# A hybrid MLA/NSA decoder in two layers: a third tile for the split weights, last down slabs in other buffers, and an earlier start of the gates

## The chip, the cores and the metric

The kernel runs on one core of a Trainium2 chip, as one program of 12504 matmuls. The metric is the device time of one execution in microseconds. The engines are named as in the profile: PE is TensorE, DVE is VectorE, ACT is ScalarE, POOL is GpSimd and SP issues transfers.

## The reference

The input is 512 tokens of width 1024. Each of two layers adds half a SwiGLU network, a token mixer, and half a second SwiGLU network; layer 0 mixes by multi-head latent attention (MLA), layer 1 by native sparse attention (NSA). One norm stands at the end.

```python
def rmsnorm(x, g):
    y = x * lax.rsqrt(jnp.mean(x * x, axis=-1, keepdims=True) + RMS_EPS)
    return y * g

def swiglu(x, w_gate, w_up, w_down):          # 1024 -> 2816 -> 1024
    return (jax.nn.silu(x @ w_gate) * (x @ w_up)) @ w_down

h = x
for i in range(2):
    h = h + 0.5 * swiglu(rmsnorm(h, ffn_norm_a[i]), ...)
    m = rmsnorm(h, mix_norm[i])
    h = h + (mla_mixer(m, ...) if i == 0 else nsa_mixer(m, ...))
    h = h + 0.5 * swiglu(rmsnorm(h, ffn_norm_b[i]), ...)
return rmsnorm(h, final_norm)
```

MLA projects to a latent of 384 for queries and 256 for keys and values, norms both, expands them to 16 heads of 64 + 32 (rotary) and applies a causal softmax. NSA has 16 heads in four groups and adds three gated branches: attention over compressed blocks of 32 tokens (an MLP over each block), over selected blocks, and over a causal window of 512 with a relative bias.

## The kernel before

**Precision and splits.** Every product is computed in fp32r (a reduced form of fp32 for PE) on values split in a high and a low part: ACT writes the high part (a copy into fp32r), DVE or POOL writes the low part (the value less the high part), and three matmuls make one product: high by high, high by low, low by high. So every weight slab that comes from memory goes through one ACT and one DVE or POOL instruction before PE may use it. `split` (L165 on) does that for activations, `wslab` (L131 on) for weights: SP loads the slab into a raw buffer `wr` (two of them), L144 writes the high part, L146 (DVE) or L150 (POOL) the low one. Both parts lie in one tile `w` from `wtiles`; there are two such tiles, by a counter, so slab number k can be written only when the matmuls that read slab k-2 are done. While `lo_pool` is set, in the two attention stages, the low parts of weights are POOL's, in pieces of up to 512 columns.

**The FFNs.** There are four, by stage a0 (5.7 to about 335 us in the trace before), b0 (546 to 895), a1 (898 to 1225) and b1 (1543 to 1860); `idx` 0 to 3 is their number. `ffn` runs over 22 blocks of 128 hidden units. The first three are "plain": 48 matmuls of 128x256 for the gate (`pg`, L365 to L367) and 48 for the up projection (`pu`). The other 19 form sums of weights and of activations (`combine`, `wsums`, `product`) and need seven products where eight stand in the plain form; the sums are DVE's work, and their tiles are `fr` (raw), `fh` and `fl` (high and low), three of each. The down projection runs in units of three blocks between those (`unit`, tiles `wdr`, `wd`), and what is left of it, the last four blocks, comes at the end of the stage, one slab of 128x512 for each of eight chunks of the residual `h`. Those eight slabs go through `wslab`, so through `wr` and `w`. In the last FFN another function, `last`, does that end.

**The norm at the start of an FFN.** The products are made of the unnormed `h`, and the norm's factor comes in afterwards. After the first plain block, `norm_col` sums squares on PE into `pc`, then a chain of twelve small DVE instructions on 128x4 (L260 to L272, the name `small`) computes the reciprocal root; `norm_bcast` (L291) spreads it over the partitions by PE into `pb`, ACT copies it to `row`, and `gate` and `act` multiply with it. All engines work in order, so PE waits at `pb` if the chain on DVE is not done.

**The attention stages.** In MLA (335 to 546 us) `query` multiplies a projection by a table into `tq` and splits it (L172) into tiles `four` and `q`; scores `s` follow, then a softmax whose last scaling is POOL's (L772), transposes `pt` and the product with the values. The output of a head pair is split into `oh` and `ol`, the low part by POOL. In NSA (1230 to 1540 us) POOL scales `p` (L1091) and the compressed branch's `e` (L1053), copies the compressed values into `vcm` (L1013), splits `ohl`, and splits the weights (L150). So POOL's queue is one list in which weight splits stand between pieces of softmax. `pp` are projections on PE, `pv` values, `ptc` the transposes of `e`.

**What sets the order.** The program is written through a tile framework. A scheduler in it puts the instructions of each engine in order by priorities and by when buffers come free. `issue_after` and `high_priority` change that. So a change of a buffer count moves instructions on every engine.

```python
t = self.first or self.wp.tile([P, 2048 + 3 * PAD], F32R, tag=f"w{self.nw % 2}", name="w")   # L128
raw = self.wp.tile([P, 1024], F32, tag="wr", bufs=2, name="wr")                              # in wslab
```

Of the kernel before, what the change touches and what calls it, by code (L numbers as in the profile page):

```python
# [11 lines left out]
F32 = mybir.dt.float32  # L12
F32R = mybir.dt.float32r
I32 = mybir.dt.int32
AF = mybir.ActivationFunctionType
# [3 lines left out]
P = 128  # L19
S = 512  # L20
D = 1024
KC = D // P
FF = 2816
NF = FF // P
EPS = 1e-6
NEG = -1e30
H = 16
# [21 lines left out]
KP = KC // 2  # L49
PLAIN = 3  # L50
PAD = 16
TILES = 24
XC = P + 2
NG = 3
# [4 lines left out]
def f32v(ap):  # L59
    return ap.bitcast(F32)  # L60


class Kern:
# [13 lines left out]
    def setup(self):  # L77
# [4 lines left out]
        self.nw, self.odd, self.nq = 0, 0, 0  # L82
        self.first = self.wp.tile([P, 2048 + 3 * PAD], F32R, tag="w0", name="w")
        small = self.wp.tile([P, 80], F32, name="small")
# [40 lines left out]

    def wtiles(self, kind="x"):

        t = self.first or self.wp.tile([P, 2048 + 3 * PAD], F32R, tag=f"w{self.nw % 2}", name="w")  # L128
        self.nw, self.first = self.nw + 1, None
        o, d = {"x": (0, 0), "act": (3 * PAD, 0), "half": (PAD, 2 * PAD)}[kind]  # L130
        return t[:, o : o + 1024], t[:, o + d + 1024 : o + d + 2048]  # L131
# [139 lines left out]
            nc.vector.tensor_tensor(t, t, y, op=ALU.mult)  # L271
            nc.vector.scalar_tensor_tensor(y, t, 1.5, y, op0=ALU.add, op1=ALU.mult)  # L272

    def norm_col(self, n, s2, pool=False):

        nc = self.nc
        pc = self.bank("o", "pc")
        for i in range(4):
            nc.tensor.matmul(pc[:, i : i + 1], s2[:, i * P : (i + 1) * P], f32v(self.ones)[:, 0:1], start=True, stop=True)
        return self.rsqrt_col(pc[:, 0:4], n, pool)  # L280

    def rsqrt_col(self, s, n, pool=False):
        v, t, col = self.vtc[:, 0:4], self.vtc[:, 4:8], self.vtc[:, 8:12]
# [85 lines left out]
    def ffn(self, idx, gain_next, ap, tp):  # L369
        nc, a = self.nc, self.a  # L370
        self.scr, self.fp = (tp, "sq", 1), tp
        ah, al, ht, row = {}, {}, [], None
        tg, tu, units = {}, {}, []

        def gate(f, g):

            t = tg[f] = tp.tile([P, S], F32, tag="tg", bufs=2, name="tg")
            nc.vector.tensor_tensor(t, g, row, op=ALU.mult)
            nc.scalar.activation(t, t, AF.Silu, scale=-1.0)
            nc.vector.tensor_tensor(t, t, row, op=ALU.mult)  # L380
# [4 lines left out]
        def act(f):  # L385
            t = tu[f]
            if f < PLAIN:
                t = tu_tile()
                nc.vector.scalar_tensor_tensor(t, tu[f], -1.0, tg[f], op0=ALU.mult, op1=ALU.mult)
            else:  # L390
                nc.vector.tensor_tensor(t, t, tg[f], op=ALU.mult)
            ah[f] = ap.tile([P, S], F32R, tag="act", bufs=4 * NG, name="ah")
            al[f] = ap.tile([P, S], F32R, tag="act", bufs=4 * NG, name="al")
            self.split(t, ah[f], al[f])

        def down(p, w, b0, b1):
            for k in range(b0, b1):
                last = self.mm3(p, w[0][:, k - b0], w[1][:, k - b0], ah[k], al[k], k == b0, k == b1 - 1)
            return last
# [27 lines left out]
                tokens(t)  # L427


        gates = [self.bank("T", "pg") for _ in range(PLAIN)]  # L430
        for f, g in enumerate(gates):
            u = tu[f] = self.bank(("mm", "S")[f % 2], "pu")
            self.plain(idx, f, 0, g)
            if f == 1 and idx == 0:

                squares(0)
                tokens(3)
                squares(1)
            if f == 2:
                pb = self.norm_bcast(col)  # L440
                row = tp.tile([P, S], F32, tag="row", bufs=1, name="row")
                nc.scalar.activation(row, pb, AF.Copy)
                for e in range(2):
                    gate(e, gates[e])
                    act(e)
            self.plain(idx, f, 1, u)
            if f == 0 and idx:
                for c in self.late:
                    self.sumsq(self.h[c])
                col = self.norm_col(D, self.s2)  # L450
            elif f == 1 and idx == 0:
                squares(2)
                squares(3)
                col = self.rsqrt_col(sums, D)
            elif f == 2:
                gate(f, g)
                act(f)
            for p in (((0,), (1,), (2, 3)) if idx else ((0, 1), (2,), (3,)))[f]:
                self.combine(p)
        t = self.tiny  # L460
# [3 lines left out]
        tail = PLAIN + (NF - 2 - PLAIN) // NG * NG  # L464
        for f in range(PLAIN, NF):
# [3 lines left out]
            n = -(-len(units) // left)  # L469
            left -= 1  # L470
            todo, units = units[:n], units[n:]
            w = self.wsums(idx, f)
            x, q, g = self.bank("S", "px")[:, :HS], self.bank("mm", "pq")[:, :HS], self.bank("T", "pg")
            uq = tp.tile([P, S], F32, tag="uq", bufs=1, name="uq")
            t = tu[f] = tu_tile()
# [18 lines left out]
        if gain_next == "fin":  # L494

            hs, out = [self.parts(self.four(F32)) for _ in range(4)], []
            for t in range(4):
                for b in range(2):
                    p = self.mm_bank("ph")
# [5 lines left out]
        self.norm_begin(gain_next)  # L505
        for c in self.order:
            p = self.mm_bank("pd")
            down(p, self.wslab(a["w_down"][idx, c, :, tail * P :], (NF - tail, P), "act"), tail, NF)
            add(c, p)
            self.norm_chunk(c)  # L510

# [130 lines left out]
    def mla(self, gain_next):  # L642
        nc, tc, a = self.nc, self.tc, self.a
        with ExitStack() as cx:
            mp = cx.enter_context(tc.tile_pool(name="mla", bufs=1, reuse_waits="tile"))
            tp = cx.enter_context(tc.tile_pool(name="mlat", bufs=2, reuse_waits="tile"))
# [12 lines left out]
            pb = self.norm_bcast(self.norm_col(D, self.s2))  # L659
            row = tp.tile([P, S], F32, tag="row", bufs=1, name="row")  # L660
# [35 lines left out]
            for k in range(2):  # L696
                nc.vector.tensor_tensor(ckv[k], ckv[k], rkv, op=ALU.mult)
                hi, lo = ckvp[2 * k : 2 * k + 2]
# [4 lines left out]
            p = self.proj(a["mla_w_in"][5], P, xh, xl, "pr")  # L703
# [47 lines left out]
            def query(h, w=None):  # L751
                p = self.proj(None, P, cqh, cql, "pq", w or query_slab(h))
                t = tp.tile([P, S], F32, tag="tq", bufs=2, name="tq")
                nc.vector.tensor_tensor(t, p, cst, op=ALU.mult)
                qh, ql = self.qtile(), self.qtile()
                self.split(t, qh, ql, pool=True)
                return qh, ql

            qs, oh, ol, o32 = {}, [], [], [None]
# [15 lines left out]
            def end(h):  # L775
                o = self.bank("o", "o")
                self.pv(o, pth[h % 2], ptl[h % 2], lambda j: vt[j][h // 4][:, h % 4, :], True, True)
                if h % 2 == 0:
                    o32[0] = tp.tile([P, S], F32, tag="o32", bufs=2, name="o32")
                self.o_out(o, o32[0], h % 2, tp)  # L780
                if h % 2 == 1:
                    hi = tp.tile([P, S], F32R, tag="o", bufs=12, name="oh")
                    lo = tp.tile([P, S], F32R, tag="o", bufs=12, name="ol")
                    self.split(o32[0], hi, lo, pool=True)
                    oh.append(hi)
                    ol.append(lo)

                if h == 0:
                    vals(1)
                if h % 2 == 1 and h + 3 < H:  # L790
                    keys((h + 3) // 2)
                if h >= 8 and h % 2 == 0:
                    self.w_o(a["mla_w_o"][0], oh[:4], ol[:4], [h // 2 - 4], False)

            w = self.wslab(a["mla_w_k"][0:2].rearrange("a p c -> p a c"), (2, 2, P))
# [538 lines left out]
```

## Time and profile before

| | |
|---|---|
| median of 3 runs | 1894.92 us (1894.47 to 1899.17) |
| the profiled execution, its own time | 1895.84 us |
| its span, first to last instruction | 1894.1 us |
| mean granted clock of PE | 0.998 |
| PE busy | 1865.5 us, 98% |
| DVE busy | 1527.9 us, 81% |
| ACT busy | 1088.9 us, 57% |
| POOL busy | 244.7 us, 13% |
| read from memory | 178.96 MB, 96 GB/s over the span |
| transfers | two hardware queues (72800 and 2944 packets); no software queue in the list |

The span is what the trace covers; the time of the execution is 1.74 us longer. A row of the trace names its line of code, engine, operation and tiles, and in brackets how long the engine was idle before it and what ended that. DVE's low parts (L146, L172) and POOL's (L150, L172) are the same operation on two engines.

### The profile page before, as it was taken

Reading aid. Unit: us, or ns where it says so; the run is one execution under the profiler, and the core shown is the slowest. Engines: PE = TensorE matmul, PEld = TensorE weight load, DVE = VectorE, ACT = ScalarE, POOL = GpSimd, SP = SyncE. Lnnn points to the kernel's source line nnn. Section 1 sums busy time; section 2 is a strip of 40 time slices with the busy share of each in tenths; the row PEclk is TensorE's granted clock in tenths of the full one; section 3 lists DMA queues with packets and bytes.
Section 4 is the critical chain, followed back from the end, with each engine's and each line's share of the span. In section 5 each row is a group of like instructions: output and inputs, shape, how many; then the busy total and the mean of one; then the engine's idle time right before and its main releaser. Section 6 shows DMA issues by size and latency. Waiting matters only on the chain.

```text
span 1894.1 us, 32916 instructions
## 1 busy us (share of the span) xinstructions
PE 1865.5 (98%) x12504; PEld 1695.8 (90%) x12504; DVE 1527.9 (81%) x2913; ACT 1088.9 (57%) x2024; POOL 244.7 (13%) x334
## 2 busy tenths in 40 slices
PE   8999999999999999999999999999989999999998
PEld 8999999878889999998999999888778889999997
DVE  8988886677778888886898878666978988888885
ACT  8555554478765555554654555436867865555553
POOL 0000000047710000000000000015656600000000
PEclk9999999999999999999999999999999999999999
DMA  6433331311132333322333332143121133333321
GB/s 237 131 101 100 102 100 41 112 53 46 60 132 90 124 101 101 102 79 86 130 124 108 105 105 75 55 141 102 51 71 64 43 115 111 111 107 104 104 77 67
DMA packets 75902, 183.26 MB, mean 97 GB/s; under 512 B 9040, under 2 KB 37072, under 8 KB 75744
## 3 DMA queue, kind: packets, MB, share of 16 engines
q1 hardware_dynamic: 72800, 176.39, 29.4%
q10 hardware_dynamic: 2944, 4.77, 0.7%
q8 instruction: 98, 1.61, 0.4%
q14 instruction: 60, 0.49, 0.1%
HBM read 178.96 MB, written 2.16 MB: 96 GB/s over the span
## 4 chain that ended last, share of the span: by engine, by line
PE 86%; DVE 6%; ACT 4%; POOL 2%; issue 1%; DMA 0%; POOLq 0%; SPq 0%; DVEq 0%; ACTq 0%
PE pd L164 8%; PE pd L165 8%; PE pd L163 8%; PE px L353 5%; PE px L354 5%; PE px L355 5%; PE pg L353 4%; PE pg L354 4%; PE pg L355 4%; PE pq L354 3%; PE pq L353 3%; PE pq L355 3%; PE o L1139 1%; PE po L164 1%; PE po L165 1%; PE po L163 1%
## 5 line engine op out<-in xcount | busy, mean ns | idle before, releaser
L164 PE MATMUL pd<-al,wd 128*128 128x512 f32 x576 | 225.3, 391 | 0.0
L163 PE MATMUL pd<-ah,wd 128*128 128x512 f32 x576 | 224.9, 390 | 0.0
L165 PE MATMUL pd<-ah,wd 128*128 128x512 f32 x576 | 224.6, 390 | 0.0
L172 DVE TENSOR_TENSOR w<-wr,w 128x1024 fp32r<-128x1024 f32 x72 | 88.2, 1224 | 123.9 <-ACT w L171 123.9
L353 PE MATMUL px<-four,wh 128*128 128x256 f32 x608 | 168.8, 278 | 0.6 <-ACT pg L478 0.6
L355 PE MATMUL px<-four,wl 128*128 128x256 f32 x608 | 168.0, 276 | 0.0
L354 PE MATMUL px<-four,wh 128*128 128x256 f32 x608 | 167.9, 276 | 0.0
L353 PE MATMUL pq<-four,wh 128*128 128x256 f32 x608 | 167.8, 276 | 0.0
L354 PE MATMUL pq<-four,wh 128*128 128x256 f32 x608 | 167.8, 276 | 0.0
L355 PE MATMUL pq<-four,wl 128*128 128x256 f32 x608 | 167.8, 276 | 0.0
L144 ACT ACTIVATE w<-wr 128x1024 fp32r<-128x1024 f32 (+5 forms) x120 | 100.7, 845 | 113.7 <-issue 25.7
L171 ACT ACTIVATE wd<-wdr 128x384 fp32r<-128x384 f32 x192 | 99.3, 519 | 98.5 <-ACT wd L171 59.1
L402 DVE SCALAR_TENSOR_TENSOR h<-pd,h 128x512 f32<-128x512 f32 x216 | 147.9, 685 | 6.9 <-PE pd L165 6.8
L165 PEld LDWEIGHTS pd<-ah,wd 128*128 128x128 f32 x576 | 108.2, 188 | 22.8
L163 PEld LDWEIGHTS pd<-ah,wd 128*128 128x128 f32 x576 | 108.1, 188 | 20.5
L164 PEld LDWEIGHTS pd<-al,wd 128*128 128x128 f32 x576 | 108.1, 188 | 19.7
L172 DVE TENSOR_TENSOR wd<-wdr,wd 128x384 fp32r<-128x384 f32 x192 | 106.1, 555 | 16.3 <-ACT wd L171 15.6
L146 DVE TENSOR_TENSOR w<-wr,w 128x1024 fp32r<-128x1024 f32 (+4 forms) x81 | 80.7, 998 | 45.1 <-ACT w L144 44.8
L640 ACT ACTIVATE p<-p,small 128x512 f32<-128x512 f32 (+2 forms) x192 | 106.5, 557 | 17.2 <-DVE small L639 14.2
L353 PEld LDWEIGHTS px<-four,wh 128*128 128x128 f32 x608 | 114.1, 188 | 2.5 <-ACT pg L478 1.9
L353 PEld LDWEIGHTS pq<-four,wh 128*128 128x128 f32 x608 | 114.2, 188 | 0.1
L354 PEld LDWEIGHTS pq<-four,wh 128*128 128x128 f32 x608 | 114.1, 188 | 0.1
(354 smaller groups left out, 6106.3 us busy)
## 6 DMA issues: line engine op xcount, KB each, us to landing
wr<-in_w_gu SPq DMA_DIRECT2D x96, 512.0 KB, 3.3
ru<-in_w_gu SPq DMA_DIRECT2D x76, 512.0 KB, 4.2
wdr<-in_w_down SPq DMA_DIRECT2D x192, 192.0 KB, 2.4
wr<-in_w_down SPq DMA_DIRECT2D x24, 256.0 KB, 2.6
wr<-in_mla_w_o SPq DMA_DIRECT2D x8, 512.0 KB, 3.4
wr<-in_nsa_w_q SPq DMA_DIRECT2D x8, 512.0 KB, 3.3
th<-btab_d SPq DMA_DIRECT2D x16, 256.0 KB, 3.5
wr<-in_nsa_w_o SPq DMA_DIRECT2D x8, 512.0 KB, 3.6
```

The costliest lines, as they stand in the source:

```text
L144: self.copied = nc.scalar.activation(wh[:, m], raw[:, m], AF.Copy)
L146: nc.vector.tensor_tensor(wl[:, m], raw[:, m], f32v(wh[:, m]), op=ALU.subtract)
L163: mm(out, wh, xh, start=first, stop=False)
L164: mm(out, wh, xl, start=False, stop=False)
L165: return mm(out, wl, xh, start=False, stop=last)
L171: nc.scalar.activation(hi, src, AF.Copy)
L172: (nc.gpsimd if pool else nc.vector).tensor_tensor(lo, src, f32v(hi), op=ALU.subtract)
L353: mm(out, wh[:, p], xh, start=first and p == 0, stop=False, skip_group_check=True)
L354: mm(out, wh[:, p], xl, start=False, stop=False, skip_group_check=True)
L355: mm(out, wl[:, p], xh, start=False, stop=last and p == KP - 1, skip_group_check=True)
L402: nc.vector.scalar_tensor_tensor(self.h[c], p, 0.5, self.h[c], op0=ALU.mult, op1=ALU.add)
L640: nc.scalar.activation(p_sb[:, :n], p_sb[:, :n], AF.Exp, bias=nm, scale=-1.0, accum_out=sm)
```

## The change

It has six parts. The program reserves 1024 bytes of each partition for dynamic transfers and not the default. `wtiles` takes three tiles in turn and not two. The last down slabs of the first three FFNs no longer go through `wslab`: the raw words go to `fr`, the parts to `fh` and `fl`, the tiles of the weight sums, at the same sizes. For `idx` 1 to 3, the two late sums of squares and the DVE chain are given a priority of 400, and `pb`, `row` and `gate` and `act` of the first two blocks (now `spread`) come before the plain gate of the third block and not after it; for `idx` 0 their place stays. In MLA, the low parts of the queries of heads 0 and 1, and of the last head pair's output, are written by DVE and not by POOL. An argument of `norm_col` that nothing used is replaced.

```diff
--- before.py
+++ after.py
@@ -49,6 +49,7 @@
 KP = KC // 2
 PLAIN = 3
 PAD = 16
+URGENT = 400
 TILES = 24
 XC = P + 2
 NG = 3
@@ -125,7 +126,7 @@
 
     def wtiles(self, kind="x"):
 
-        t = self.first or self.wp.tile([P, 2048 + 3 * PAD], F32R, tag=f"w{self.nw % 2}", name="w")
+        t = self.first or self.wp.tile([P, 2048 + 3 * PAD], F32R, tag=f"w{self.nw % 3}", name="w")
         self.nw, self.first = self.nw + 1, None
         o, d = {"x": (0, 0), "act": (3 * PAD, 0), "half": (PAD, 2 * PAD)}[kind]
         return t[:, o : o + 1024], t[:, o + d + 1024 : o + d + 2048]
@@ -271,13 +272,14 @@
             nc.vector.tensor_tensor(t, t, y, op=ALU.mult)
             nc.vector.scalar_tensor_tensor(y, t, 1.5, y, op0=ALU.add, op1=ALU.mult)
 
-    def norm_col(self, n, s2, pool=False):
+    def norm_col(self, n, s2, urgent=0):
 
         nc = self.nc
         pc = self.bank("o", "pc")
         for i in range(4):
             nc.tensor.matmul(pc[:, i : i + 1], s2[:, i * P : (i + 1) * P], f32v(self.ones)[:, 0:1], start=True, stop=True)
-        return self.rsqrt_col(pc[:, 0:4], n, pool)
+        with self.tc.high_priority(urgent) if urgent else nullcontext():
+            return self.rsqrt_col(pc[:, 0:4], n)
 
     def rsqrt_col(self, s, n, pool=False):
         v, t, col = self.vtc[:, 0:4], self.vtc[:, 4:8], self.vtc[:, 8:12]
@@ -369,7 +371,7 @@
     def ffn(self, idx, gain_next, ap, tp):
         nc, a = self.nc, self.a
         self.scr, self.fp = (tp, "sq", 1), tp
-        ah, al, ht, row = {}, {}, [], None
+        ah, al, ht = {}, {}, []
         tg, tu, units = {}, {}, []
 
         def gate(f, g):
@@ -427,27 +429,33 @@
                 tokens(t)
 
 
+        def spread():
+            pb = self.norm_bcast(col)
+            nc.scalar.activation(row, pb, AF.Copy)
+            for e in range(2):
+                gate(e, gates[e])
+                act(e)
+
+        row = tp.tile([P, S], F32, tag="row", bufs=1, name="row")
         gates = [self.bank("T", "pg") for _ in range(PLAIN)]
         for f, g in enumerate(gates):
             u = tu[f] = self.bank(("mm", "S")[f % 2], "pu")
+            if f == 2 and idx:
+                spread()
             self.plain(idx, f, 0, g)
+            if f == 2 and idx == 0:
+                spread()
             if f == 1 and idx == 0:
 
                 squares(0)
                 tokens(3)
                 squares(1)
-            if f == 2:
-                pb = self.norm_bcast(col)
-                row = tp.tile([P, S], F32, tag="row", bufs=1, name="row")
-                nc.scalar.activation(row, pb, AF.Copy)
-                for e in range(2):
-                    gate(e, gates[e])
-                    act(e)
             self.plain(idx, f, 1, u)
             if f == 0 and idx:
-                for c in self.late:
-                    self.sumsq(self.h[c])
-                col = self.norm_col(D, self.s2)
+                with self.tc.high_priority(URGENT):
+                    for c in self.late:
+                        self.sumsq(self.h[c])
+                col = self.norm_col(D, self.s2, URGENT)
             elif f == 1 and idx == 0:
                 squares(2)
                 squares(3)
@@ -505,7 +513,11 @@
         self.norm_begin(gain_next)
         for c in self.order:
             p = self.mm_bank("pd")
-            down(p, self.wslab(a["w_down"][idx, c, :, tail * P :], (NF - tail, P), "act"), tail, NF)
+            raw = tp.tile([P, D], F32, tag="fr", bufs=3, name="wdr")[:, : (NF - tail) * P]
+            nc.sync.dma_start(raw, a["w_down"][idx, c, :, tail * P :])
+            w = [t[:, : (NF - tail) * P].rearrange("p (k c) -> p k c", c=P) for t in self.sum_tiles(1024)]
+            self.split(raw.rearrange("p (k c) -> p k c", c=P), *w)
+            down(p, w, tail, NF)
             add(c, p)
             self.norm_chunk(c)
 
@@ -753,7 +765,7 @@
                 t = tp.tile([P, S], F32, tag="tq", bufs=2, name="tq")
                 nc.vector.tensor_tensor(t, p, cst, op=ALU.mult)
                 qh, ql = self.qtile(), self.qtile()
-                self.split(t, qh, ql, pool=True)
+                self.split(t, qh, ql, pool=h > 1)
                 return qh, ql
 
             qs, oh, ol, o32 = {}, [], [], [None]
@@ -781,7 +793,7 @@
                 if h % 2 == 1:
                     hi = tp.tile([P, S], F32R, tag="o", bufs=12, name="oh")
                     lo = tp.tile([P, S], F32R, tag="o", bufs=12, name="ol")
-                    self.split(o32[0], hi, lo, pool=True)
+                    self.split(o32[0], hi, lo, pool=h + 1 < H)
                     oh.append(hi)
                     ol.append(lo)
 
@@ -1321,7 +1333,7 @@
     from concourse.bass_utils import run_bass_kernel_spmd
 
     arrays = _layout({k: np.asarray(v) for k, v in inputs.items()}) | _constants()
-    nc = bacc.Bacc("TRN2", target_bir_lowering=False, num_devices=1)
+    nc = bacc.Bacc("TRN2", target_bir_lowering=False, num_devices=1, dynamic_dma_scratch_size=1024)
     args, feed = {}, {}
     for name, v in arrays.items():
         feed[f"in_{name}"] = v
```

**POOL in NSA.** The copies `vcm` (L1013 before, L1025 after) with the weight splits (L150, then L151) around them, and the softmax's scaling (L1091, then L1103) behind. Before:

```order
L150 TENSOR_TENSOR w<-wr,w 128x512 x2
L1013 TENSOR_SCALAR vcm_14127<-vc 32x128 x4
L1013 TENSOR_SCALAR vcm_14128<-vc 32x128 x4
L1013 TENSOR_SCALAR vcm_14129<-vc 32x128 x4
L1013 TENSOR_SCALAR vcm_14130<-vc 32x128 x4
L150 TENSOR_TENSOR w<-wr,w 128x512 x4
L1091 TENSOR_SCALAR p<-p,small,gat 128x256 x4
```

After:

```order
L151 TENSOR_TENSOR w<-wr,w 128x512 x4
L1025 TENSOR_SCALAR vcm_14151<-vc 32x128 x4
L1025 TENSOR_SCALAR vcm_14152<-vc 32x128 x4
L1025 TENSOR_SCALAR vcm_14153<-vc 32x128 x4
L1025 TENSOR_SCALAR vcm_14154<-vc 32x128 x4
L151 TENSOR_TENSOR w<-wr,w 128x512 x4
L1103 TENSOR_SCALAR p<-p,small,gat 128x256 x4
```

One slab of 1024 columns (two pieces of 512) more is split ahead of the copies. Behind them the places of the splits are the same up to the fourth `e`, each with the next slab in it; at the fourth `e` (L1053, then L1065) the list before is

```order
L1091 TENSOR_SCALAR p<-p,small,gat 128x512
L150 TENSOR_TENSOR w<-wr,w 128x512
L1053 TENSOR_TENSOR e<-e,small 128x512
L150 TENSOR_TENSOR w<-wr,w 128x512
L1091 TENSOR_SCALAR p<-p,small,gat 128x512
```

and the list after

```order
L1103 TENSOR_SCALAR p<-p,small,gat 128x384
L1103 TENSOR_SCALAR p<-p,small,gat 128x512
L1065 TENSOR_TENSOR e<-e,small 128x512
L1103 TENSOR_SCALAR p<-p,small,gat 128x512
L1103 TENSOR_SCALAR p<-p,small,gat 128x384 x2
```

The two halves of a slab around `e` are no longer there.

**DVE in the MLA opening.** `cst` is the query's table with the norm in it (L801, then L813), `tq` the query before its split (L754, then L766), L639 (then L651) the softmax's maximum. Before:

```order
L801 TENSOR_TENSOR cst<-cst,row 128x512
L754 TENSOR_TENSOR tq<-pq,cst 128x512 x3
L639 ISA p,small<-s,mask 128x512
L639 ISA small 128x1
L639 ISA p,small<-s,mask 128x384
```

After:

```order
L813 TENSOR_TENSOR cst<-cst,row 128x512
L766 TENSOR_TENSOR tq<-pq,cst 128x512 x2
L173 TENSOR_TENSOR four<-tq,four 128x512
L173 TENSOR_TENSOR four<-tq,q 128x512
L766 TENSOR_TENSOR tq<-pq,cst 128x512
L651 ISA p,small<-s,mask 128x512
```

The two splits, POOL's before, stand between the second and the third `tq`.

**PE at the start of the last FFN.** The four `pb` stand among the matmuls of the plain blocks. Before, between the third block's gate and its up projection:

```order
L366 MATMUL pg<-x,w 128x256
L367 MATMUL pg<-x,w 128x256
L291 MATMUL pb<-ident,small 128x128 x4
L365 MATMUL pu<-x,w 128x256
L366 MATMUL pu<-x,w 128x256
```

After, between the second block's up projection and the third block's gate:

```order
L368 MATMUL pu<-x,w 128x256
L369 MATMUL pu<-x,w 128x256
L293 MATMUL pb<-ident,small 128x128 x4
L367 MATMUL pg<-x,w 128x256
L368 MATMUL pg<-x,w 128x256
```

They moved ahead of 48 matmuls, as in the two FFNs before it.

## The prediction

> **What bounds the kernel now.** I read the page first, then the waits of TensorE, then the busy time by window, and last the single instructions at each wait.
>
> ```profile
> span 1894.1 us, 32916 instructions
> PE 1865.5 (98%) x12504; PEld 1695.8 (90%) x12504; DVE 1527.9 (81%) x2913; ACT 1088.9 (57%) x2024; POOL 244.7 (13%) x334
> PE 86%; DVE 6%; ACT 4%; POOL 2%; issue 1%; DMA 0%; POOLq 0%; SPq 0%; DVEq 0%; ACTq 0%
> ```
>
> TensorE is busy for 1865.5 of 1894.1 us, and no DMA ends the chain of waits. The change leaves the arithmetic as it is, so it can win only what lies in the 28.6 us of idle time, in a lower clock, and in nothing else. The waits of TensorE by line and releaser (in total, times, longest) say where that idle time is:
>
> ```profile
> PE ptc L1058 <- POOL e L1053: 4.1, 4, 2.4
> PE pv L164 <- POOL w L150: 1.7, 2, 1.0
> PE pg L353 <- ACT pg L485: 1.2, 3, 0.8
> PE pv L163 <- ACT w L144: 0.7, 1, 0.7
> PE s L165 <- POOL four L172: 0.6, 1, 0.6
> PE po L164 <- POOL ol L172: 0.6, 1, 0.6
> PE pp L165 <- POOL w L150: 0.6, 1, 0.6
> ```
>
> Five of these seven lines end on POOL, though POOL is busy 13% of the span: late splits of weights, of queries and of `o`, and a late `e`, in the two attention stages. The two that end on ACT are late sums in the FFNs (`pg` L353) and a late high half of a weight (`pv` L163). By window (from:to, length, then busy PE, PEld, DVE, ACT, POOL, then the granted clock, the DMA share and GB/s):
>
> ```profile
> 47.00:331.00 284.00, 283.97 (x2027) 264.79 (x2026) 234.16 (x361) 143.07 (x236) 0.00 (x0) 1.00 0.31 96
> 400.00:412.00 12.00, 10.83 (x57) 8.33 (x56) 7.71 (x27) 10.05 (x25) 11.14 (x12) 1.00 0.13 46
> 540.00:546.00 6.00, 5.37 (x25) 4.06 (x24) 3.21 (x5) 3.29 (x6) 1.28 (x1) 1.00 0.51 175
> 603.00:607.00 4.00, 3.81 (x31) 3.44 (x31) 4.00 (x7) 2.17 (x4) 0.00 (x0) 1.00 0.00 0
> 935.00:939.00 4.00, 3.82 (x29) 3.29 (x28) 4.00 (x6) 3.13 (x8) 0.00 (x0) 1.00 0.00 0
> 1304.00:1308.00 4.00, 3.41 (x16) 2.50 (x15) 1.97 (x6) 1.97 (x3) 3.67 (x7) 1.00 0.24 82
> 1381.00:1390.00 9.00, 6.54 (x34) 5.61 (x34) 6.50 (x23) 6.50 (x19) 6.30 (x7) 0.81 0.27 88
> 1386.10:1389.50 3.40, 3.09 (x13) 3.06 (x14) 2.19 (x9) 1.67 (x7) 1.84 (x3) 0.50 0.47 157
> 1408.00:1413.00 5.00, 2.62 (x20) 2.19 (x19) 3.64 (x14) 3.29 (x9) 4.80 (x6) 1.00 0.31 105
> 1471.00:1475.00 4.00, 3.08 (x20) 2.50 (x19) 3.55 (x12) 3.20 (x8) 4.00 (x5) 1.00 0.00 0
> 1585.00:1589.00 4.00, 3.80 (x32) 3.49 (x31) 4.00 (x8) 2.34 (x4) 0.00 (x0) 1.00 0.01 2
> 1601.00:1605.00 4.00, 3.21 (x26) 2.97 (x25) 3.09 (x6) 2.81 (x4) 0.00 (x0) 1.00 0.57 182
> 1612.00:1615.00 3.00, 2.84 (x25) 2.65 (x24) 3.00 (x5) 1.65 (x3) 0.00 (x0) 1.00 0.13 46
> ```
>
> The first row is the steady part of an FFN: 283.97 of 284.00 us busy at the full clock. Nothing is to be won there, whatever moves. The costliest place is 1381 to 1390: 2.46 us idle, and the only lowered clock of these rows, 0.50 for 3.40 us.
>
> Idle time understates a stall a little. The times at which TensorE goes from the second plain `up` to the third `gate`, and the end of the norm's chain on VectorE ahead of it, for the FFNs b0, a1 and b1:
>
> ```profile
> 582.83 0.15 DVE L272 SCALAR_TENSOR_TENSOR small<-small 128x4 f32<-128x4 f32 x1
> 583.46 0.28 PE L367 MATMUL pu<-x,w 128*128 128x256 f32 x1
> 583.57 0.28 PE L365 MATMUL pg<-x,w 128*128 128x256 f32 x1
> 920.59 0.15 DVE L272 SCALAR_TENSOR_TENSOR small<-small 128x4 f32<-128x4 f32 x1
> 921.19 0.28 PE L367 MATMUL pu<-x,w 128*128 128x256 f32 x1
> 1564.48 0.15 DVE L272 SCALAR_TENSOR_TENSOR small<-small 128x4 f32<-128x4 f32 x1
> 1565.63 0.28 PE L367 MATMUL pu<-x,w 128*128 128x256 f32 x1
> 1567.37 1.23 DVE L146 TENSOR_TENSOR w<-wr,w 128x1024 fp32r<-128x1024 f32 x1 [1.19 <-ACT w L144]
> 1572.48 1.23 DVE L172 TENSOR_TENSOR w<-rg,w 128x1024 fp32r<-128x1024 f32 x1 [3.88 <-ACT w L171]
> ```
>
> Successive matmuls start 0.11 us apart (583.46, 583.57) while each record lasts 0.28, so a stall delays TensorE by about 0.16 us more than the idle time that it shows. I add that once for each stall.
>
> **The change, part by part.**
>
> *Third weight tile, NSA.* A slab no longer waits for the matmuls of the slab two before it. By the order of POOL's instructions the place directly ahead of the `vcm` copies now holds two slabs instead of one, and from there on each place holds the split of the next slab; the last one, split in two halves around the fourth `e`, is gone. What POOL does at those places now:
>
> ```profile
> 1299.79 5.67 POOL L1013 TENSOR_SCALAR vcm<-vc 32x128 fp32r<-32x128 f32 x16 [1.55 <-DVE vc L172]
> 1305.55 5.04 POOL L150 TENSOR_TENSOR w<-wr,w 128x512 fp32r<-128x512 f32 x4
> 1371.44 2.58 POOL L150 TENSOR_TENSOR w<-wr,w 128x512 fp32r<-128x512 f32 x2
> 1383.39 2.97 POOL L150 TENSOR_TENSOR w<-wr,w 128x512 fp32r<-128x512 f32 x2
> 1471.02 1.32 POOL L150 TENSOR_TENSOR w<-wr,w 128x512 fp32r<-128x512 f32 x1
> 1472.28 1.06 POOL L1053 TENSOR_TENSOR e<-e,small 128x512 f32<-128x512 f32 x1
> ```
>
> The slab that `pp` waits for near 1307 is split behind 5.67 us of `vcm`; ahead of them it has been done for over 5 us. The value slab that `pv` waits for is split from 1383.39 on; at the place of 1371.44 (ended at 1374.02) it is done 7 us before the window of these waits begins, so the stalls and the drop of the clock after them have no cause left. POOL's other work keeps its places and its load, so its scaling of `p` is not later. Ahead of the fourth `e` a 1.32 us half is gone. The three gains:
>
> 1304 to 1308: 0.59 + 0.16 = 0.75. 1381 to 1390: 2.46 + 3 x 0.16 = 2.94, and the clock, half of 3.40 = 1.70, together 4.64. 1471 to 1475: 0.92 + 0.16 = 1.08. Sum 6.5. The gap at 1408 to 1413 (2.38 idle) stays: a slab's split still stands directly ahead of that `e`.
>
> *Reserve for dynamic transfers.* It only frees memory for the tile: 0. SP's DMA issues move, but the rows above give DMA no part in any chain.
>
> *Last down slabs in other buffers.* The splits stay of the same kind and size, so their cost is 0; the first slabs of the next stage are now loaded and split before the last downs end. TensorE does not wait at those seams now, so I count no gain. It costs if a raw buffer is late for the tail; the nearest row is a whole split, 1.23 us, at three seams (the last FFN has no such slabs), so the bound is 0 to +3.7. I take 0, since the tail's slabs rotate through three buffers where they had two.
>
> *`pb`, `row` and the first two gates ahead of the third plain `gate`.* TensorE does the same 48 matmuls in another order (0), and VectorE gets its first `tg` one plain earlier, 48 x 0.113 = 5.4 us, in b0, a1 and b1. Today VectorE is idle there, 1.19 + 3.88 us in b1 (the two last rows above), and then lags: in the windows at 603, 935, 1585 and 1612 it is busy without a break while TensorE waits, and at 1601, the largest, for 3.09 of 4.00. With 5 us of work pulled into that hole a lag of under 1 us should not remain: 0.19 + 0.18 + 0.20 + 0.79 + 0.16 idle, and 5 x 0.16, make 2.3.
>
> *The chain "ahead" on VectorE.* In the order the chain's twelve small instructions stand between the same slab splits as before, so it is not shorter: 0. But its cover falls: `pb` could come 5.4 us late without harm, and now TensorE asks for it right after the last `pu`, 0.6, 0.6 and 1.1 us after the chain's end in b0, a1 and b1 (the rows above: end of L272 against the last `pu` start plus 0.11). If that cover is gone it costs what the chain is late, in each of three stages, since TensorE keeps its order and the third `gate` stands behind `pb`. I take 0, because every margin is above none and nothing new stands ahead of the chain; the bounds are 0 and 3 x (1.22 - 0.6) = 1.9, one slab's split more ahead of it.
>
> *Splits from POOL to VectorE.* Two query splits in the MLA opening and the last head pair's `ol`:
>
> ```profile
> L172 DVE TENSOR_TENSOR wl<-s,wh 128x512 fp32r<-128x512 f32 x76 | 52.1, 686 | 0.0
> L172 POOL TENSOR_TENSOR ol<-o,oh 128x512 fp32r<-128x512 f32 x8 | 10.3, 1293 | 16.4 <-ACT oh L171 16.4
> ```
>
> A split takes 0.69 us there instead of 1.29, so `po` comes 0.6 us earlier (0.6 of its 0.63 us), and the first scores 1.2 us earlier, of which 0.63 + 0.16 were waited, and a little behind them: 1.0. VectorE is idle for 4.29 of the 12.00 us from 400 to 412, so 2 x 0.69 fit; the third `tq` stands behind them, and its scores come after the first head's. The 0.53 us left in that window, a wait for POOL's `p`, stays.
>
> Sum: 6.5 + 2.3 + 1.6 = 10.4. A removed stall may leave a rest where the next input was not far behind; over these twelve stalls I allow 0.9, which is my choice and no row's. That gives -9.5 us. The profiled execution took 1895.84 us, the median of the three runs is 0.92 us less; so 1895.84 - 9.5 = 1886.3 by the profile and **1885.4** by the median.
>
> **The Trainium skill against the trace.** "TensorE: Matmul & The Clock Gate", section "HAM oscillation — how this bites in real kernels", has the clock fall only for idle gaps over about 3.4 us, judged in windows that run freely. The trace shows less: 2.46 us idle, in three pieces, preceded the drop at 1386, and 2.38 us in one piece at 1408 had none. So the trace does not agree with that length: by the rule neither should have dropped, and the 1.70 would not be won with the stalls. I keep it in the sum because the drop stands right behind the only such sequence of waits; without it the sum gives 1887.1. That the phase of the windows counts speaks for the first rival below.
>
> **Rivals.**
>
> *The drop of the clock moves.* With other stalls gone, the gap at 1408, as long as the one that dropped the clock, may meet the gate at a worse phase. It costs 1.70: 1887.1. For it: the two idle sums, 2.46 and 2.38, are alike. Against it: the gap stands alone, with full work around it.
>
> *The raw words bind, not the tiles.* A slab's raw buffer, of which there are still two, is free only when POOL has split it. If the value slab's words or its high half on ACT come too late for POOL's earlier place, POOL waits with its queue of `p` behind it, and the gain of NSA, 6.5, falls to between 0 and 3.3: -3.0 to -6.3, about 1890. For it: POOL ends five waits. Against it: two slabs' splits, 2.6 and 3.0 us long, stand 12 us apart (1371.44, 1383.39), so a buffer is long free.
>
> *Slower: `pb` waits for the chain.* If the chain ends 3.5 us later than now (three slab splits of 1.22 us more ahead of it), TensorE stands 3.5 us in b0, a1 and b1, each long enough for the lowered clock at 1.70: 3 x 5.2 = 15.6 against 9.5 gained, 1901. It ends slower than before from (9.5 / 3) - 1.70 = 1.5 us a stage if the clock drops with it, from 3.2 us if not. For it: all margins are at or under 1.1 us. Against: the order puts nothing new ahead of the chain.
>
> *More than the sum.* If the gap at 1408 goes as well, with no rest: -10.4 - (2.38 + 0.16), against the median 1882.0.
>
> **How the numbers follow.** The forecast has 0.55 (1885.4, alone 1883 to 1888.5), the moved drop 0.13, the raw words 0.20, more than the sum 0.06, slower 0.06. A difference within 0.3% (5.7 us, so down to 1889.2) cannot be told from none. Faster: 0.52 of the forecast, 0.12 of the moved drop, 0.06 of more than the sum and 0.06 of the raw words, 0.76; same: what is left of these, 0.18; slower: 0.06. The range is 1881 to 1891.5: it takes in the larger gain and most of the raw words, and leaves out their end at -3.0 and the slow case.
>
> **What would show it.** Right: in NSA `pv` and `pp` have no wait for POOL's `w`, and the clock is 1.00 throughout; `s` and `po` have none for POOL; `pg` L353 none for ACT in b0, a1, b1; the gap before the third `e` remains. Wrong: an idle TensorE before `pb`, ended by the chain's last instruction; a slab's split on POOL with a long wait for ACT ahead of it; a lowered clock at another place; waits of TensorE at the seams after the last down slabs.

## The result, and the profile after

The changed kernel takes 1917.64 us (median of 4 runs, 1916.32 to 1918.13), the kernel before 1895.37 in the same comparison: a ratio of 1.0113, 95% interval 1.0095 to 1.0130. It is 22 us slower where 9.5 us less were forecast, and far outside the range. Three runs behind these times and the ones below, one of the kernel before and two of one variant, had a granted clock of 0.63 to 0.75 and took 2313 to 3237 us; they are in no median.

The page of the changed kernel:

```profile
span 1916.3 us, 32818 instructions
PE 1890.0 (99%) x12504; PEld 1722.3 (90%) x12504; DVE 1538.3 (80%) x2916; ACT 1073.8 (56%) x2024; POOL 242.0 (13%) x331
```

TensorE executes the same 12504 matmuls, but is busy for 1890.0 us instead of 1865.5, while its idle time fell from 28.6 to 26.3 us. So the time was not lost in waits. Some of its waits (total, times, longest):

```profile
PE ptc L1070 <- POOL e L1065: 3.1, 3, 2.4
PE s L164 <- DVE small L651: 1.7, 5, 0.7
PE px L355 <- ACT pg L486: 1.7, 2, 1.3
PE pg L355 <- ACT pg L493: 0.9, 1, 0.9
PE s L166 <- DVE four L173: 0.5, 1, 0.5
```

The waits of `pv` and `pp` for POOL's weights are gone, as forecast, and so is the fourth wait of `ptc`. What was lost instead shows only in how many matmuls fit into busy time. The same 200 us of the first FFN, of the kernel before:

```profile
100.00:300.00 200.00, 200.00 (x1438) 187.19 (x1437) 167.76 (x260) 103.08 (x169) 0.00 (x0) 1.00 0.32 99
```

and of the changed kernel:

```profile
100.00:300.00 200.00, 200.00 (x1413) 187.70 (x1412) 164.89 (x253) 98.36 (x166) 0.00 (x0) 1.00 0.32 100
```

TensorE is busy without a break in both, at the full granted clock (1.00), and gets through 1413 matmuls instead of 1438. The single matmuls say where: before,

```profile
200.63 0.28 PE L353 MATMUL px<-four,wh 128*128 128x256 f32 x1
200.97 0.28 PE L353 MATMUL px<-four,wh 128*128 128x256 f32 x1
201.31 0.28 PE L353 MATMUL px<-four,wh 128*128 128x256 f32 x1
201.65 0.28 PE L353 MATMUL px<-four,wh 128*128 128x256 f32 x1
```

and after,

```profile
202.50 0.28 PE L355 MATMUL px<-four,wh 128*128 128x256 f32 x1
202.85 0.28 PE L355 MATMUL px<-four,wh 128*128 128x256 f32 x1
203.20 0.29 PE L355 MATMUL px<-four,wh 128*128 128x256 f32 x1
203.56 0.28 PE L355 MATMUL px<-four,wh 128*128 128x256 f32 x1
```

Each row stands three matmuls behind the one above it: 1.02 us for nine before, 1.06 after, that is 113 and 118 ns from one start to the next. The duration of a record does not show it; the distance of starts does. Over all of the trace, I took for each matmul the time to the next start less the usual time for its columns, the median before (113 ns for 256, 227 for 512, 177 for 384, 109 for 128). Gaps with over 0.2 us of excess add up to 22.6 us before and 18.8 after; all the smaller ones to 26.6 before and 52.6 after. So the waits won 3.8 us, and the pace lost 26. (The first expectation below has 27.2 and 53.2 for the smaller gaps, by a slightly different count; the difference is the same.)

By stage, from the first `pu` of an FFN to its last `pd`, and what lies between (us, from the starts of matmuls in the profiled executions; "aligned" is the first experiment below):

| stage | before | after | aligned |
|---|---|---|---|
| FFN a0 | 334.8 | 342.6 | 334.4 |
| MLA | 220.4 | 221.7 | 220.6 |
| FFN b0 | 331.9 | 338.2 | 332.2 |
| FFN a1 | 331.5 | 339.2 | 332.2 |
| NSA | 312.9 | 306.4 | 307.4 |
| FFN b1 | 337.2 | 342.7 | 336.7 |

All four FFNs became 5.5 to 7.8 us longer, the first too, in whose start hardly anything was moved.

### The profile page after: what moved, and what is told of

Same layout as the page of the kernel before. It is cut to its first block, busy times and chain, and to the rows that moved or that the text cites. A ratio compares the mean times of both kernels' runs of the same rounds, so it can differ in the third digit from the quotient of the medians.

```text
span 1916.3 us, 32818 instructions
## 1 busy us (share of the span) xinstructions
PE 1890.0 (99%) x12504; PEld 1722.3 (90%) x12504; DVE 1538.3 (80%) x2916; ACT 1073.8 (56%) x2024; POOL 242.0 (13%) x331
## 5 line engine op out<-in xcount | busy, mean ns | idle before, releaser
L355 PE MATMUL px<-four,wh 128*128 128x256 f32 x608 | 171.7, 282 | 1.7 <-ACT pg L486 1.7
L356 PE MATMUL px<-four,wh 128*128 128x256 f32 x608 | 171.1, 281 | 0.0
L355 PE MATMUL pq<-four,wh 128*128 128x256 f32 x608 | 170.9, 281 | 0.0
L356 PE MATMUL pq<-four,wh 128*128 128x256 f32 x608 | 170.5, 280 | 0.0
L173 DVE TENSOR_TENSOR wl<-s,wh 128x512 fp32r<-128x512 f32 x76 | 52.5, 691 | 146.2 <-ACT wh L172 146.2
L145 ACT ACTIVATE w<-wr 128x1024 fp32r<-128x1024 f32 (+5 forms) x96 | 85.4, 897 | 88.8 <-PE po L166 18.4
L172 ACT ACTIVATE wh<-s 128x512 fp32r<-128x512 f32 x76 | 47.9, 631 | 152.2 <-PE px L356 144.3
L355 PEld LDWEIGHTS px<-four,wh 128*128 128x128 f32 x608 | 115.0, 189 | 2.1 <-ACT pg L486 2.1
L357 PEld LDWEIGHTS px<-four,wl 128*128 128x128 f32 x608 | 115.1, 189 | 0.0
L356 PEld LDWEIGHTS px<-four,wh 128*128 128x128 f32 x608 | 114.8, 189 | 0.0
L355 PEld LDWEIGHTS pq<-four,wh 128*128 128x128 f32 x608 | 114.6, 188 | 0.0
```

The lines of the kernel that those rows point to most:

```text
L145: self.copied = nc.scalar.activation(wh[:, m], raw[:, m], AF.Copy)
L172: nc.scalar.activation(hi, src, AF.Copy)
L173: (nc.gpsimd if pool else nc.vector).tensor_tensor(lo, src, f32v(hi), op=ALU.subtract)
L355: mm(out, wh[:, p], xh, start=first and p == 0, stop=False, skip_group_check=True)
L356: mm(out, wh[:, p], xl, start=False, stop=False, skip_group_check=True)
L357: mm(out, wl[:, p], xh, start=False, stop=last and p == KP - 1, skip_group_check=True)
```

## The experiments

**What the memory looks like.** A new theory had to explain slower starts of the same matmuls. The built programs give each tile's place in a partition. A weight tile `w` has 2096 words, 8384 bytes, which is 65.5 times 128. Two of them take 131 x 128 bytes; a third one moves every tile behind it by 64 bytes modulo 128. Before, `x` and `four` (the moving operands of the FFNs) start at a multiple of 128 bytes, and the weights' sums `wh` and `wl` at 64 behind one. After, both start at a multiple of 128, and the third `w` stands in the other half than the first two. Theory A: a 128x256 matmul starts every 113 ns if weights and moving operand stand 64 bytes apart modulo 128, and every 118 to 119 ns otherwise. Rival B: the new order, fuller queues, or other engines at the memory slow TensorE. Rival C: the smaller reserve.

**The aligned kernel.** Only a gap ahead of the third tile is added to the changed kernel:

```diff
+        if self.nw == 2 and self.first is None:
+            self.wp.tile([P, 16], F32, tag="gap", bufs=1, name="gap")
         t = self.first or self.wp.tile([P, 2048 + 3 * PAD], F32R, tag=f"w{self.nw % 3}", name="w")
```

> The changed kernel with one unused tile of 64 bytes a partition ahead of the third weight tile, so that this tile starts at a multiple of 128 bytes and every tile behind it lies 64 bytes further, as in the kernel before. Instructions, waits and order are those of the changed kernel. Theory A (place in memory: a 128x256 matmul is started every 113 ns where its weights and its moving operand lie in different halves of 128 bytes, and every 118 to 119 ns where they lie in the same half): the 26 us by which the short gaps between starts grew (53.2 us after against 27.2 before, all single gaps under 0.3 us) go away: 1917.6 - 26 = 1891.6, range 1889 to 1894, with 128x256 starts back at 113 ns. Rival B (the new order, crowded queues or engines that share memory with TensorE): it stays within 3 us of 1917.6.

Measured: 1889.61 us, ratio to the kernel before 0.9968 (0.9956 to 0.9980). The same window:

```profile
100.00:300.00 200.00, 200.00 (x1443) 187.34 (x1442) 168.68 (x258) 100.58 (x171) 0.00 (x0) 1.00 0.33 105
```

64 unused bytes took away the whole loss, 28 us (ratio 1.0113 to 0.9968), and the starts on `four` and `wh` are back at 113 ns (the table below). The order, the queues and the work of every engine are those of the changed kernel, so rival B is out.

**The kernel before, made slow.** The same gap in it, behind its two tiles (no third tile):

> The kernel before, with 64 unused bytes a partition behind its two weight tiles; nothing else differs, and the order is that of the kernel before. Theory A: the weight sums' parts (wh, wl) move into the half in which four and x lie; 3648 matmuls on four and 912 on x at some 5.2 ns more each make +24 us: 1919, range 1914 to 1923. Rival B (order, queues, engines): no instruction moved, so 1895.4, within 0.3%.

Measured: 1921.0 us, ratio 1.0131 (1.0114 to 1.0148), and 1406 matmuls where there were 1438:

```profile
100.00:300.00 200.00, 200.00 (x1406) 187.66 (x1405) 163.21 (x253) 101.88 (x165) 0.00 (x0) 1.00 0.31 98
```

The gap alone, with no instruction moved, costs 24.9 us. The changed kernel loses some 3 us more to its places, and has a third `w` in the other half: its 128x256 matmuls on `x` and `w` start every 116.1 ns on the mean, and every 114.6 in the aligned kernel, which over 2946 of them is about 4 us, by an estimate from these means.

**The reserve alone.** `dynamic_dma_scratch_size=1024` in the kernel before:

> The kernel before with only the smaller reserve for dynamic transfers: every tile lies 15360 bytes lower, a multiple of 128. Theory A: 1895.4, no change (within 0.2%). Rival C (the smaller reserve or the move by kilobytes is itself what costs): between 1900 and 1918.

Measured: 1895.6 us, ratio 1.0001 (0.9992 to 1.0010). Rival C is out; a move by a multiple of 128 bytes costs nothing.

**Relative or absolute.** In the kernel before, the gap stands ahead of `x` and `four`, so that activations and weights move together:

```diff
         self.h = [self.hp.tile([P, S], F32, name=f"h{c}") for c in range(KC)]
+        self.hp.tile([P, 16], F32, name="gap")
```

> The kernel before with 64 unused bytes a partition ahead of the tiles x and four: activations, weights and sums all lie 64 bytes further, so the halves of weights against those of moving operands stay as before wherever both are moved. Theory A in its relative form (it matters whether both lie in the same half): 1895.4, within 0.3%. Theory A in its absolute form (weights must lie in the odd half): about as slow as the kernel with 64 bytes behind the weight tiles, 1919.

Measured: 1896.08 us, ratio 0.9995 (0.9986 to 1.0005). So a place as such does not count, only places relative to each other.

**32 bytes.** As the second experiment, with a gap of 8 words:

> The kernel before with 32 unused bytes behind its two weight tiles, so that wh, wl and wd lie 96 bytes behind a multiple of 128 (x and four at 0). If a half of 64 bytes decides: the weights stay in the odd half, 128x256 starts stay at 113 ns, 1896 (within 0.3%). If the two streams must stand a whole 64 bytes apart: part of the 5 to 6 ns is lost at 4560 matmuls, 1905 to 1921.

Measured: 1920.55 us, ratio 1.0129 (1.0116 to 1.0143). A distance of 96 bytes costs as much as one of 0; my idea of "halves" was wrong, of the distances tried only 64 is fast. The mean time from start to start of the matmuls on `four` with `wh`, over gaps under 140 ns:

| kernel | weights behind `four`, modulo 128 bytes | ns per start | ratio of times |
|---|---|---|---|
| before | 64 | 113.4 | 1 |
| all moved by 64 | 64 | 113.4 | 0.9995 |
| aligned | 64 | 113.3 | 0.9968 |
| after | 0 | 118.6 | 1.0113 |
| weights moved by 64 | 0 | 119.2 | 1.0131 |
| weights moved by 32 | 96 | 118.3 | 1.0129 |

One group does not fit. The 912 matmuls of `px` on `x` and `w` have a distance of 64 in the kernel before, in the aligned one and in the one with its weights moved by 64; they start every 117.2 ns in the first two and every 115.0 in the third. So the distance of a matmul's own two operands is not all of it; what else counts was not tried.

**The third tile alone,** with reserve and gap, the other parts left out:

> The kernel before with the smaller reserve, the third weight tile and the 64 bytes that keep the halves; the other four parts of the change left out. If the stalls of NSA were the third tile's alone, as the prediction has it: 1896.1 - 5.5 (what the NSA stage shows as gained in the aligned kernel) = 1890.6, range 1889 to 1892, with no wait of pp or pv for POOL's w. Rival: the tile alone gives little, because the next slabs come too late without the last down slabs' move; then 1894 to 1896.

Measured: 1891.7 us, ratio 0.9972 (0.9961 to 0.9984). NSA fell from 312.9 to 308.0 in its trace, without a wait of `pp` or `pv` for POOL. But MLA grew from 220.4 to 225.7, in a profiled execution that was the longest of nine (1895.84 us). Its waits there, and POOL in the same place:

```profile
398.05 1.88 PE L293 MATMUL pb<-ident,small 128*128 128x128 f32 x8 [1.86 <-DVE small L274]
407.36 0.68 PE L167 MATMUL s<-four 128*128 128x512 f32 x2 [2.20 <-POOL four L174]
```

```profile
403.57 2.52 POOL L152 TENSOR_TENSOR w<-wr,w 128x512 fp32r<-128x512 f32 x2 [5.68 <-ACT w L146]
406.04 1.27 POOL L174 TENSOR_TENSOR four<-tq,four 128x512 fp32r<-128x512 f32 x1
407.26 1.30 POOL L174 TENSOR_TENSOR four<-tq,q 128x512 fp32r<-128x512 f32 x1
```

In the kernel before, POOL had them in the other order:

```profile
401.23 1.28 POOL L172 TENSOR_TENSOR four<-tq,four 128x512 fp32r<-128x512 f32 x1
402.46 1.29 POOL L172 TENSOR_TENSOR four<-tq,q 128x512 fp32r<-128x512 f32 x1
405.23 2.55 POOL L150 TENSOR_TENSOR w<-wr,w 128x512 fp32r<-128x512 f32 x2
```

With a tile free, the weight slab (2.52 us) is put ahead of the first query's split on POOL, and the first scores wait 2.20 us where they waited 0.63. The clock also fell twice there in that execution:

```profile
398.00:402.00 4.00, 3.95 (x14) 3.51 (x15) 1.29 (x2) 0.60 (x1) 0.00 (x0) 0.57 0.43 150
408.00:412.00 4.00, 4.00 (x16) 3.38 (x14) 2.46 (x10) 3.90 (x8) 2.82 (x3) 0.57 0.00 0
```

That is 4.00 x 0.43 = 1.7 us each time, so about 1.9 of the 5.3 us are the later splits and norm; the median of the nine is 4.1 us below this execution, so the drops were probably not in most of them.

**The parts undone one by one,** each in the aligned kernel. The query's and the last `o`'s low parts back on POOL:

```diff
-                self.split(t, qh, ql, pool=h > 1)
+                self.split(t, qh, ql, pool=True)
-                    self.split(o32[0], hi, lo, pool=h + 1 < H)
+                    self.split(o32[0], hi, lo, pool=True)
```

> The aligned changed kernel (64 unused bytes), with the low parts of the first queries and of the last o back on POOL. By the prediction (they gain 1.6 us): 1889.6 + 1.6 = 1891.2. By the trace of the aligned kernel (MLA takes 220.6 us where it took 220.4; new waits of the first scores for VectorE's splits and softmax): no loss, 1889.0 to 1889.8.

Measured: 1893.85 us, ratio 0.9981 (0.9972 to 0.9991), MLA 222.0 us instead of 220.6. The interval meets that of the aligned kernel; the stage's trace says 1.4 us, near the 1.6 forecast.

`pb`, `row` and the first gates back behind the third plain gate (`spread()` called there for every `idx`):

> The aligned changed kernel with pb, row and the first two gates back behind the third plain gate in all FFNs. By the prediction (2.3 us gained in b0, a1, b1): 1889.6 + 2.3 = 1891.9. By the trace of the aligned kernel (the three FFNs together are as long as before, the early stalls partly replaced by others): 1889.6, within 1.

Measured: 1893.22 us, ratio 0.9981 (0.9971 to 0.9990). The stages b0, a1 and b1 take 332.4, 333.8 and 337.0 us instead of 332.2, 332.2 and 336.7: 2.1 us, where 2.3 were forecast. The sum, 1003.2, lies 1.7 to 2.3 above those of the three profiles that have this order and the new tails (1000.9, 1001.1 and 1001.5), so the term is clear of their spread. Here too the intervals of the times overlap.

The last down slabs back in `wr` and `w`:

> The aligned changed kernel with the last down slabs back in the raw and weight tiles. By the prediction (this part costs and gains 0): 1889.6. By the matmuls on those slabs (192 of 288 start every 232 to 234 ns where they started every 227): 192 x 6 ns = 1.1 us back, 1888.5, with these matmuls at 227 ns.

Measured: 1890.44 us, ratio 0.9966 (0.9954 to 0.9978), a0, b0 and a1 at 333.9, 331.3 and 331.2 us instead of 334.4, 332.2 and 332.2. Once more, with more rounds:

> The aligned changed kernel with the last down slabs back in the raw and weight tiles, once more, with more rounds. By its trace (FFNs b0 and a1 0.9 and 1.0 us shorter than in the aligned kernel, a0 0.5): 0.9955 to 0.9965 of the kernel before.

Measured: 1890.5 us, ratio 0.9965 (0.9953 to 0.9978), the three stages at 334.2, 331.4 and 331.9. So that part of the change costs 1.3 to 2.4 us by the traces, a size that is near their spread (b0, a1 and b1 add up to 999.1 and 999.9 us here, and to 1000.9 to 1001.5 with the new tails); the times alone do not tell this kernel from the aligned one.

**The tail's matmuls.** In the aligned kernel the low parts of these slabs stand 128 bytes into their tile. Without that:

```diff
-            w = [... for t in self.sum_tiles(1024)]
+            w = [self.fp.tile([P, 1024 + z], F32R, tag=t, bufs=3, ...)[:, : (NF - tail) * P]... for t, z in (("fh", 0), ("fl", 2 * PAD))]
```

> The aligned changed kernel with the low parts of the last down slabs at the start of their tile and not 128 bytes into it. In all traces so far a 128x512 matmul starts every 227 ns where weights and moving operand differ by a multiple of 256 bytes, and every 232 to 234 where by 128. If that is the cause of the 192 slow tail matmuls: these at 227 ns and 1.1 us less than the aligned kernel, 1888.5; if not, they stay at 232 to 234.

Measured: 1890.06 us, ratio 0.9969 (0.9957 to 0.9981). The starts of `pd<-al,wh` and `pd<-ah,wl` went from 231.1 and 232.2 to 228.1 and 228.6 ns on the mean: 96 x (3.0 + 3.6) ns = 0.6 us of the 1.1 expected. The direction holds. The rule does not explain all of it: in the built aligned kernel `al` and `wh` stand at distance 0, and they were slow. And 0.6 us is below what the times can tell.

**Two tiles in MLA, three elsewhere,** on the kernel with the down slabs back in their tiles (the tiles' names in a list, one of which is held back from the first keys of MLA to the end of its attention):

> As the kernel beside it, and two weight tiles instead of three from the first keys of MLA to the end of its attention. If the third tile is what lengthened the MLA opening (weight splits ahead of the query's on POOL, 2.4 us waited for the first scores where two tiles had 0.8), and VectorE's query splits then gain what was predicted: the MLA stage 218.8 us instead of 220.6, in all 1.8 us less than the kernel beside it. If the third tile is not the cause: the same time as beside it.

Measured: 1889.41 us, ratio 0.9966 (0.9954 to 0.9978), MLA 220.3 us against 220.7. By the gaps between starts, the waits of the first scores (0.66 and 0.84 us) are gone and that of the norm's `pb` fell from 1.18 to 0.43, but only 0.4 of 1.8 us came of it: the transposes at 408.62 now wait 1.05 us instead of 0.38, and at 525.08 stands a gap of 0.88 that the kernel beside it does not have. That the third tile caused the wait for the first scores is borne out; that MLA would be shorter by it is not. Why the other waits came up was not tried.

The changed kernel with the gap, and the variants on it, with all its parts or without the down slabs', are some 0.3% faster than the kernel before, and so faster than both; between 0.9965 and 0.9969 the times do not choose.

## Why the prediction was wrong

**The step that failed** is the sentence that the change "leaves the arithmetic as it is, so it can win only what lies in the 28.6 us of idle time, in a lower clock, and in nothing else". In the sum, the third tile was priced by waits alone; that it moves every tile behind it had no term. (The reserve's own 0 was right: its run is at 1.0001.) I took the time of a matmul as fixed by its shape. The steady row, 283.97 of 284.00 us busy, was read as "Nothing is to be won there, whatever moves"; it was never asked what could be lost there. The places of the two operands relative to each other set the pace of most of the 128x256 matmuls, and the odd length of the third tile moved the sums' tiles to the slow distance: 26 us by the gaps between starts, 28 by the gap experiment. The kernel's own offsets in `w`, `fl` and `u` are multiples of `PAD`, 16 words or 64 bytes, and were the one hint that could be read ahead. None of the rivals had this; the slow one, `pb` waiting for the chain, did not happen: in the FFNs of the changed kernel the first `pb` starts 0.12 us behind the matmul ahead of it. Nor could the signs listed under "What would show it" have warned. Those of being right held in the changed kernel but for one wait of `pg` for ACT, 0.9 us, and it was slower all the same: they look at waits and at the clock, and the pace is neither.

**The rest of the sum,** by the aligned kernel, where pace is out of the way: 6.5 us less (1889.61 against 1896.12; by the interval of the ratio, 3.8 to 8.3) against the 9.5 forecast.

- *NSA, 6.5 forecast, 4.8 of it waits.* 312.9 to 307.4, 5.5 us, where the clock fell in both. Where it did not, 305.9 to 306.4, against 311.3 in the kernel before with all moved by 64: 4.9 to 5.4. The mechanism was right: the splits moved ahead by one slab and the waits went. That the changed kernel's own profile shows the full 6.5 (306.4) is luck with the clock.
- *The clock.* It was right to give the moved drop a chance, and wrong to book 1.70 as won. The drop was not even a fixed part of the kernel before: with all moved by 64, the same instructions in the same order show the same idle time at the same place, 2.45 us, at the full clock:

```profile
1381.00:1390.00 9.00, 6.55 (x44) 5.50 (x43) 7.73 (x22) 6.33 (x16) 5.82 (x7) 1.00 0.15 45
```

  In the aligned kernel it fell at the gap that was to stay:

```profile
1380.00:1392.00 12.00, 12.00 (x89) 11.15 (x88) 10.36 (x40) 10.05 (x31) 8.13 (x11) 1.00 0.22 68
1400.00:1416.00 16.00, 13.63 (x79) 11.81 (x79) 12.17 (x38) 12.37 (x28) 10.80 (x11) 0.89 0.28 95
```

  The first window holds the old place of the drop, now busy throughout; the second one has it, 16.00 x 0.11 = 1.8 us.
- *FFNs, 2.3 forecast.* The term itself measured 2.1. But b0, a1 and b1 together are no shorter than before (1001.1 against 1000.6 us): the last down slabs, priced at 0, cost 1.1 to 1.9 us in b0 and a1, and new waits came up late in the stages (in the changed kernel `px` and `pg` for ACT, 1.7 and 0.9 us in the waits above). In the third-tile kernel a1 takes 332.6 us instead of 331.5, but the three stages together 1000.5, as before, and a1 alone differs by 1.6 us between the three profiles with the old tails in the aligned kernel (331.2, 331.9, 332.8). So whose these waits are is not shown.
- *MLA, 1.6 forecast.* The splits on DVE measured 1.4, but against a worse start: the third tile first put a weight slab ahead of the query's split and cost about as much. I had priced each part against the kernel before, and not against the kernel with the other parts in it.
- *`pb` behind a shorter cover, 0 forecast.* It held in all three FFNs.

## What to carry to other kernels

A change of a buffer count or of any size is also a change of every address behind it. Before it is priced by waits, compare the places of the operands of the hottest matmuls modulo 128 and 256 bytes in both programs; and if a kernel is slower with the same waits, look at the distance of starts, not at busy shares. Give odd-sized tiles a filler, so that a count can be changed without moving the rest.

Price the parts of a change in the order in which they act on each other: a gain of one part was here the repair of another's loss.

## What the runs showed of the hardware

In these kernels the 128x256 matmuls in fp32r on `four` and the weights' sums start every 113 ns where weights and moving operand stand 64 bytes apart modulo 128 in their partitions, and every 118 to 119 ns on the mean at distances of 0 and 96. Both operands moved together by 64 bytes change nothing (ratio 0.9995). The `px` on `x` and `w`, 115 to 117 ns at a distance of 64, do not fit, and what in the memory does this is not shown by these runs. For 128x512 matmuls a distance of 64 does no good: those on `wd` with `ah` and `al` start every 227.9 and 228.6 ns at distance 0 in the kernel before, and the tail's on `w` went from 226.7 at distance 0 to 227.5 (`ah`) and 231.7 (`al`) where the distance became 64.

The granted clock can fall to half, for 3.4 us each time, around a gap of TensorE of 2.4 us, and need not: of the fourteen profiles nine show such a drop between start and end, and five none. It came even behind 1.86 us in one piece (the wait of `pb` in the third-tile kernel). The same kernel, with the last down slabs in their old tiles, had it in one profile

```profile
1400.00:1416.00 16.00, 13.63 (x77) 11.88 (x76) 11.79 (x40) 11.98 (x31) 10.93 (x13) 0.89 0.31 99
```

and not in the next:

```profile
1400.00:1416.00 16.00, 13.62 (x88) 11.85 (x87) 13.05 (x46) 13.47 (x34) 12.26 (x14) 1.00 0.32 98
```

The busy time is the same, 13.63 and 13.62 of 16.00 us. The Trainium skill, "TensorE: Matmul & The Clock Gate", section "HAM oscillation — how this bites in real kernels", names idle gaps over about 3.4 us as the condition. The two rows do not agree with that length, since the gap here is 2.4 us (and 1.86 us was enough above); that the windows run freely, as the page's section "What's actually happening" has it, agrees with a drop that one execution has and the next does not.
